# A hybrid attention and recurrence block on one core: the three parked operands of a recurrence head are fetched together instead of one after the other

## The chip, the cores and the metric

The kernel runs on one core of a Trainium2 chip. Its time is the device time of one execution in microseconds (us); lower is better. Besides the time there is one profiled execution, whose trace gives for every instruction its engine, start and duration, and for a waiting engine what it waited for. The engines are PE (matrix multiplication; PEld is its weight load), DVE (vector), ACT (scalar), POOL and SP. A DMA is issued by an engine's instruction queue (SPq, ACTq, POOLq): the issuing instruction stands in the engine's program order with everything else that the engine does.

## The reference

One layer over 512 tokens and 16 meta tokens, model width 2048:

```python
h = rms_norm(x, norm_g)
proj = h @ w_in                       # 2048 -> 12368 columns
(q_a, k_a, v_a, z_a, q_i, k_i, w_i, q_b, f_b, i_b, z_b, gates) = split(proj)
...
o_a = dsa_attention(q, k, v, qi, ki, wi, chunk_ids, topk)     # branch A, 8 heads
y_a = o_a * silu(z_a)
qb = silu(q_b); f = lb + (1 - lb) * sigmoid(f_b); vb = i_b    # branch B, 8 heads of 128
o_b = rms_norm(hgrn2_chunkwise(qb, 1 - f, vb, log(f)), hgrn_out_norm_g)
y_b = o_b * silu(z_b)
merged = sum over the branches of sigmoid(gates) * (y @ w_branch)
return x + merged @ w_out
```

Branch B is a gated linear recurrence: S_t = diag(f_t) S_{t-1} + k_t v_t^T, o_t = S_t^T q_t. For each head it needs the three projections f, q and v, and, after the recurrence, z.

## The kernel before, in words

**Matrix products.** Weights stream from HBM in blocks of 128x1024 elements (tiles `raw`, 512 KB each, a ring of six, DMAs on SP's queue, L381). Each block is split into a high part (`wh`, on ACT, L106) and a low part (`wl`, on DVE, L112), which PE multiplies with the equally split activations. Most blocks belong to pairs: two column groups of 128 are computed with seven block products instead of eight (`run_pair`, L1267). The products carry the names of their PSUM banks: px, py, pv, pz, pw. Sums of weight blocks are made on DVE or by an accumulating DMA on POOL's queue (`raw<-raw`, L121). A product is 24 matmuls of some 256 columns.

**Tasks between the products.** The work that is not a weight product (index scores, top-k, the recurrence, the attention) is written as Python generators, `Task` (L205). A planner (`pump`, L229) is called after every third matmul of a product. It keeps a planned clock for each engine, and lets a task take its next step when the time that the task last yielded, plus a margin of 300 ns, has passed on PE's planned clock. So a yield does not wait on the chip: it decides at build time behind which matmuls the task's next instructions are written. On the chip each engine runs its instructions in that order and waits for semaphores.

**The pairs' order.** First 16 pairs for the recurrence (two for each head: f and q, then v and z), two for the attention's z, eight for the attention's q, k and v, and 16 for the gates; then the products with `w_branch` and `w_out`.

**Parked operands.** SBUF holds 71 tiles of 128x528 (`Slots`). When an operand of a later task is ready and fewer than eight tiles are free, `hold` (L809) writes it to DRAM (tile `held`, on SP's queue, L800) and frees its tile; otherwise it stays. `held` (L817) brings it back: it waits until the store has been written into the program, until a tile is free, then issues the load on ACT's queue (`fetch`, L803, whose DMA line in the profile is L805), and yields the time at which the planner takes it as landed, 4.0 us after the issue on PE's planned clock.

**The recurrence's task.** `hgrn_task` (L981) of head h starts when that of head h-1 is done. It gets f, q and v with three calls of `held`, one behind the other (L984 to L986). Then it transposes v on PE (rows `phl<-ident` and `phv<-ident`; the operand is printed as v, or as r where it was not parked), makes k = 1 - f on ACT (`hk<-f`) and q*f on DVE (`QA<-q,f`), multiplies k and q on PE (`phd`), and goes through seven levels on PE and DVE (`phl<-QA,hk`), a state update (`phs`) and the output (`pho`). The gate of a finished head (`gate_task`, L1105) fetches that head's z in the same way. The attention's tasks `ka_task` and `va_task` fetch xk and xv; they begin when the recurrence's last head is done, the softmax part `pv_task` (`pov`) comes behind them. When the eighth `pv_task` is done, `y_task` loads the branch outputs back (`yr`, on ACT's queue).

Of the kernel before, what the change touches and what calls it, by code (L numbers as in the profile page):

```python
# [30 lines left out]
WAIT = object()  # L31
# [157 lines left out]
def hybrid_kernel(ctx, tc, x, meta, vecs, w_in, rows, w_branch, w_out,  # L189
                  ident_d, tab_q, tab_a, tab_i, masks_d, out):  # L190
    nc = tc.nc
# [5 lines left out]
    E = Core(nc)  # L197
# [70 lines left out]
    def room(n, first=False):  # L268
        while len(S.free) < n + (0 if first else keep[0]):
            yield WAIT  # L270
# [6 lines left out]
    def slot(name, dt=F32):  # L277
        return S.get(name, dt)
# [23 lines left out]
    for c in range(2):  # L302
        s = wp.tile([128, 1024], F32, name=f"xm{c}", tag=f"wh{c}")
# [499 lines left out]
    def fetch(name, of, q, n=512):  # L803
        s = slot(name)
        q.dma_start(s[:, :n], of[:, :n])  # L805
        E.wr[s.tensor.name] = (E.clk["pe"] + 4000.0, "dma")
        return s
# [9 lines left out]
    def held(name, x):  # L817
        s, d, t, n = x
        if s is None:
            while not t.done:  # L820
                yield WAIT
            yield from room(1)
            s = fetch(name, d, nc.scalar, n)
            yield E.wr[s.tensor.name][0]
        return s

    small = [cp.tile([128, 16], F32, name=f"small{i}") for i in range(2)]
    SC = 128.0 ** -0.5

# [137 lines left out]
    hg = {}  # L967
# [13 lines left out]
    def hgrn_task(h, prev):  # L981
        while not LB or not mask_t[0].done or (prev and not prev.done):
            yield WAIT
        f = yield from held("f", hg[h]["f"])  # L984
        q = yield from held("q", hg[h]["q"])
        vx = yield from held("v", hg[h]["v"])  # L986
        yield from room(3)
        at = AT[0]
        k, vt = slots("hk", 2)
# [4 lines left out]
        for c in range(4):  # L994
            e = E.tr(pb[:, 128 * c:128 * c + 128], vx[:, 16 + 128 * c:144 + 128 * c], ident)
# [8 lines left out]
        for c in range(4):  # L1004
            e = E.mm(pb[:, 128 * c:128 * c + 128], k[:, 16 + 128 * c:144 + 128 * c], q[:, 128 * c:128 * c + 128],
                     True, True)
# [7 lines left out]
        for li, m in enumerate(LEVELS):  # L1014
# [5 lines left out]
            for c in range(4):  # L1020
                for j in range(128 // w):
                    e = E.mm(pb[w * j:w * j + ns, 64 * c + w // 2 * j:64 * c + w // 2 * (j + 1)],
                             k[:, 16 + 128 * c + w * j:16 + 128 * c + w * j + ns],
                             qv[:, (128 * c + w * j) // (2 * m):(128 * c + w * j) // (2 * m) + nr, 1, :], True, True)
# [8 lines left out]
            if m < 16:  # L1033
                kv = k[:, :528]
                n = 528 // m
                roff = 16 // m
            else:
                kv = k[:, 16:528]
                n = 512 // m
# [7 lines left out]
            e = E.tt(qv[:, :, 1, :], qv[:, :, 1, :], tr_[:, :, 0:1].to_broadcast([128, 256 // m, m]), OP.mult)  # L1047
            e = E.tt(tt_[:, nxt:nxt + n // 2], tv[:, :, 0], tv[:, :, 1], OP.mult)
# [6 lines left out]
        for c in range(3):  # L1055
            e = E.tr(pb[:, 128 * c:128 * c + 128], k[:, 16 + 128 * c:144 + 128 * c], ident)
# [4 lines left out]
        e = E.act(kd[:, :384], pb[:, :384], AF.Copy)  # L1061
# [4 lines left out]
        for c in range(3):  # L1066
            e = E.mm(pb[:, 128 * c + 128:128 * c + 256], kd[:, 128 * c:128 * c + 128],
                     vt[:, 128 * c:128 * c + 128], True, True)
# [4 lines left out]
        for c in range(3):  # L1073
            e = E.stt(ss[:, 128 * c + 128:128 * c + 256], ss[:, 128 * c:128 * c + 128],
                      tt_[:, toff + c:toff + c + 1], pb[:, 128 * c + 128:128 * c + 256], OP.mult, OP.add)
# [4 lines left out]
        for c in range(4):  # L1080
            cs = slice(128 * c, 128 * c + 128)
            E.mm(po[:, cs], at[:, cs], vt[:, cs], True, False)
            e = E.mm(po[:, cs], qa[:, cs], ss[:, cs], False, True)
# [5 lines left out]
        r = sq[:, 512:528]  # L1089
# [3 lines left out]
        e = E.ptt(r[:, 8:12], r[:, 4:8], mhalf[:, 0:4], OP.pow)  # L1093
        yield e
        e = E.tt(on[:, :512].rearrange("p (b d) -> p b d", b=4), pv, r[:, 8:12, None].to_broadcast([128, 4, 128]),
                 OP.mult)
# [77 lines left out]
    def r_ib(h):  # L1174
        def f(s):
            hg[h]["v"] = hold(s)
            hg_tasks.append(spawn(hgrn_task(h, hg_tasks[-1] if hg_tasks else None), 1))
        return f
# [599 lines left out]
    for u, un in enumerate(units):  # L1778
        d = int(un[1])
# [64 lines left out]
    for half in range(2):  # L1844
        n = (272, 256)[half]
# [154 lines left out]
```

## Time and profile before

| | us |
|---|---|
| median of three runs | 1530.59 |
| lowest and highest of them | 1528.60 and 1531.83 |
| the profiled execution's own time | 1529.07 |
| its span from the first to the last instruction | 1527.3 |
| PE busy in that span | 1500.9 |
| DVE, ACT, POOL busy | 1201.0, 712.5, 165.9 |

The span and the busy times are read from the head of the page; a busy time sums the instructions of one engine, so the difference to the span is the time in which that engine did nothing. For PE that is 26.4 us. The granted clock of PE was 0.999 of full speed over the whole span.

### The profile page before, as it was taken

What the parts mean: (1) busy time and instruction counts of PE and PEld (TensorE: products, weight loads), DVE (VectorE), ACT (ScalarE), POOL (GpSimd) and SP (SyncE); (2) the same over time, 40 slices, a digit from 0 to 9 for tenths busy, and PEclk for the clock granted to TensorE, in tenths of its full rate; (3) what the DMA queues carried; (4) which work ended last, traced back from release to release, by engine and by line L of the source; (5) the groups of instructions that cost most, each with busy time, mean ns of one, the idle gap of its engine ahead of it and who ended that gap; (6) DMA issues with size and microseconds to landing.
All of it is one profiled execution on the core that took longest, in us unless ns stands there. A gap on an engine that the chain in (4) does not pass through costs nothing.

```text
span 1527.3 us, 31296 instructions
## 1 busy us (share of the span) xinstructions
PE 1500.9 (98%) x12756; PEld 1435.2 (94%) x12756; DVE 1201.0 (79%) x2013; ACT 712.5 (47%) x1079; POOL 165.9 (11%) x180
## 2 busy tenths in 40 slices
PE   7999999999999999999999999999999999999998
PEld 6888889999999999999999999999999799989998
DVE  6699899999977787787768768768756768898765
ACT  5565444444434444434554554554454544444342
POOL 2100010010001001011101101101010000002221
PEclk9999999999999999999999999999999999999999
DMA  9323448766666585758677677676678767748883
GB/s 266 83 70 83 110 103 196 187 168 166 162 172 164 148 190 137 185 131 198 142 192 181 156 192 180 161 191 166 164 203 195 228 188 188 212 123 217 214 214 90
DMA packets 300288, 256.50 MB, mean 168 GB/s; under 512 B 11828, under 2 KB 262208, under 8 KB 300144
## 3 DMA queue, kind: packets, MB, share of 16 engines
q1 hardware_dynamic: 271392, 177.44, 40.0%
q0 software_dynamic: 15616, 56.71, 21.3%
q10 hardware_dynamic: 13136, 20.35, 4.2%
q8 instruction: 100, 1.64, 0.5%
q14 instruction: 44, 0.36, 0.1%
HBM read 169.11 MB, written 28.73 MB: 130 GB/s over the span
## 4 chain that ended last, share of the span: by engine, by line
PE 86%; DVE 8%; DMA 2%; issue 2%; ACT 2%; ACTq 0%; SPq 0%; POOL 0%; DVEq 0%
PE pz L96 16%; PE px L96 16%; PE pg L98 12%; PE po L96 10%; PE pv L96 8%; PE pw L96 8%; PE py L96 8%; DVE wl L112 2%; PE phl L98 1%; PE pov L96 1%; PE psc L98 1%; PE plg L98 1%; PE pho L98 1%; ACT wh L106 1%; DVE tk L697 1%
## 5 line engine op out<-in xcount | busy, mean ns | idle before, releaser
L106 ACT ACTIVATE wh<-raw 128x1024 fp32r<-128x1024 f32 x416 | 440.1, 1059 | 557.7 <-PE pz L96 148.9
L112 DVE TENSOR_TENSOR wl<-raw,wh 128x1024 fp32r<-128x1024 f32 x414 | 508.3, 1228 | 148.1 <-ACT wh L106 144.7
L121 POOL DMA_DIRECT2D raw<-raw x108 | 95.0, 993 | 969.0 <-DVE raw L112 678.3
L96 PE MATMUL px<-hH,wh 128*128 128x272 f32 (+1 forms) x672 | 194.6, 290 | 1.3 <-ACT p L106 1.3
L96 PE MATMUL px<-hL,wh 128*128 128x272 f32 (+1 forms) x672 | 192.1, 286 | 0.0
L96 PE MATMUL px<-hH,wl 128*128 128x272 f32 (+1 forms) x672 | 192.1, 286 | 0.0
L96 PE MATMUL po<-wh,mh 128*128 128x256 f32 x896 | 158.5, 281 | 0.5 <-DVE xq L112 0.5
L96 PEld LDWEIGHTS po<-wh,mh 128*128 128x128 f32 x896 | 137.3, 189 | 0.8 <-DVE xq L112 0.7
L112 DVE TENSOR_TENSOR raw<-raw,raw 128x1024 f32<-128x1024 f32 x108 | 132.0, 1222 | 1.8
L96 PEld LDWEIGHTS px<-hH,wh 128*128 128x128 f32 x672 | 126.9, 189 | 2.1 <-ACT p L106 1.6
L96 PEld LDWEIGHTS px<-hL,wh 128*128 128x128 f32 x672 | 126.9, 189 | 0.0
L96 PEld LDWEIGHTS px<-hH,wl 128*128 128x128 f32 x672 | 126.8, 189 | 0.0
L96 PE MATMUL pw<-tT,wh 128*128 128x256 f32 x672 | 126.4, 287 | 0.0
L96 PE MATMUL po<-wl,mh 128*128 128x256 f32 x448 | 125.7, 280 | 0.0
L96 PE MATMUL pv<-tT,wh 128*128 128x256 f32 x672 | 125.1, 285 | 0.0
L96 PE MATMUL pz<-tT,wh 128*128 128x256 f32 x672 | 124.3, 284 | 0.2 <-ACT wh L106 0.2
L96 PEld LDWEIGHTS pz<-tT,wh 128*128 128x128 f32 x672 | 103.2, 189 | 0.9 <-ACT wh L106 0.4
L96 PEld LDWEIGHTS pv<-tT,wh 128*128 128x128 f32 x672 | 103.0, 189 | 0.5
L96 PEld LDWEIGHTS pw<-tT,wh 128*128 128x128 f32 x672 | 103.1, 189 | 0.2
L96 PE MATMUL pz<-hH,wh 128*128 128x256 f32 x336 | 97.3, 289 | 2.9 <-DVE r L112 2.9
L96 PE MATMUL py<-hH,wl 128*128 128x256 f32 x336 | 94.8, 282 | 1.9 <-DVE wl L112 1.9
L96 PE MATMUL py<-hH,wh 128*128 128x256 f32 x336 | 95.9, 286 | 0.0
(349 smaller groups left out, 3582.9 us busy)
## 6 DMA issues: line engine op xcount, KB each, us to landing
raw<-in_w_in_dram SPq DMA_DIRECT2D x192, 512.0 KB, 6.1
raw<-raw POOLq DMA_DIRECT2D x108, 512.0 KB, 6.0
raw<-in_w_branch_dram SPq DMA_DIRECT2D x32, 512.0 KB, 6.3
raw<-in_w_out_dram SPq DMA_DIRECT2D x32, 512.0 KB, 6.5
gd<-r SPq DMA_DIRECT2D x32, 256.0 KB, 2.0
gate<-gd SPq DMA_DIRECT2D x32, 256.0 KB, 6.2
held<-r SPq DMA_DIRECT2D x19, 264.0 KB, 4.0
held<-r SPq DMA_DIRECT2D x18, 256.0 KB, 2.0
```

The lines of the kernel that those rows point to most:

```text
L96: self.nc.tensor.matmul(out, lhsT, rhs, start=start, stop=stop, skip_group_check=True)
L98: self.nc.tensor.matmul(out, lhsT, rhs, start=start, stop=stop)
L106: self.nc.scalar.activation(out, in_, f, **kw)
L112: self.nc.vector.tensor_tensor(out, a, b, op=op)
L121: self.nc.gpsimd.dma_start(out, a, accum_op=OP.add)
L697: e = E.dve([w], [src, m8], kq, lambda v: v.match_replace(w, m8, src, NEG))
```

## The change

A new helper gets any number of parked operands at once. It waits until the stores of all of them stand in the program and until as many tiles are free as operands are parked, issues all loads on ACT's queue one directly behind the other, and yields once, with the latest of their planned landing times.

```diff
+    def held_all(*xs):
+        for _, (s, d, t, n) in xs:
+            while s is None and not t.done:
+                yield WAIT
+        yield from room(sum(x[0] is None for _, x in xs))
+        r, e = [], 0.0
+        for name, (s, d, t, n) in xs:
+            if s is None:
+                s = fetch(name, d, nc.scalar, n)
+                e = max(e, E.wr[s.tensor.name][0])
+            r.append(s)
+        yield e
+        return r
...
     def hgrn_task(h, prev):
         while not LB or not mask_t[0].done or (prev and not prev.done):
             yield WAIT
-        f = yield from held("f", hg[h]["f"])
-        q = yield from held("q", hg[h]["q"])
-        vx = yield from held("v", hg[h]["v"])
+        f, q, vx = yield from held_all(("f", hg[h]["f"]), ("q", hg[h]["q"]), ("v", hg[h]["v"]))
         yield from room(3)
```

ACT's queue at the start of the recurrence's head 1, before: L805 are the loads of parked operands (f, q and v of this head, z of head 0), `wh` the high parts of weight blocks, `r` and `p` evictions of pair products.

```order
L805 DMA f_3684<-held_3012 128x528
L805 DMA z_3686<-held_2689 128x512
L106 ACTIVATE wh_3691<-raw_3385 128x1024
L106 ACTIVATE r_278_3694<-px_3578 128x272
L106 ACTIVATE wh_3727<-raw_3387 128x1024
L805 DMA q_3753<-held_2971 128x512
L106 ACTIVATE wh_3770<-raw_3421 128x1024
L106 ACTIVATE wh_3804<-raw_3464 128x1024
L805 DMA v_3810<-held_3330 128x528
```

The same place on ACT in the changed kernel:

```order
L805 DMA f_3679<-held_3029 128x528
L805 DMA q_3681<-held_2991 128x512
L805 DMA v_3683<-held_3342 128x528
L805 DMA z_3685<-held_2689 128x512
L106 ACTIVATE wh_3693<-raw_3389 128x1024
L106 ACTIVATE r_280_3696<-px_3585 128x272
L106 ACTIVATE wh_3731<-raw_3391 128x1024
L106 ACTIVATE hk_3755<-f_3679 128x528
```

q now stands directly behind f instead of four instructions after it, and v two behind f instead of eight. The first use of f (`hk`) is three instructions behind the last load, with two weight blocks in between; before, it came only in row 291 of ACT, 13 behind f, with six weight blocks in between. The line of the load is L805 in both, since the new helper stands behind it.

PE's queue where that head's v is transposed, before (`phl` and `phv` are the transposes, `py` a pair's product):

```order
L96 MATMUL py_3881<-hH_265,wl_3805 128x256
L102 MATMUL phl_2452<-ident,v_3810 16x128
L102 MATMUL phv_3889<-ident,v_3810 128x128 x4
L96 MATMUL py_3881<-hH_289,wh_3804 128x256
L96 MATMUL py_3881<-hL_290,wh_3804 128x256
```

And in the changed kernel, where the same transposes stand in an earlier product, `pz` of the weight block `wh_3652`:

```order
L96 MATMUL pz_3734<-tT_1778,wl_3653 128x256
L102 MATMUL phl_2452<-ident,v_3683 16x128
L102 MATMUL phv_3758<-ident,v_3683 128x128 x4
L102 MATMUL pht_3766<-ident,on_3550 128x128 x4
L96 MATMUL pz_3734<-tT_1949,wh_3652 128x256
```

The transposes have moved from PE's row 1980 to its row 1903, and the transpose of head 0's output (`pht`) has come to stand beside them. All of the recurrence moves so, by more with every head: v of head 7 is transposed in row 4133 before and in row 3810 now, and the attention's last `pov` moves from row 7725 to 7583. From row 7738 on PE's rows are the same in both. PE has 10587 rows in both programs, DVE 1895 and POOL 185; ACT has 1103 instead of 1104 and SP 424 instead of 425, because one operand less is parked over the whole kernel (36 instead of 37). Of the recurrence's 24 operands 18 are fetched in either program: eight f, six q and four v before, five f, six q and seven v now. Before, ten loads waited for another load of the same head; now none does.

## The prediction, made before the changed kernel ran

> **What bounds the kernel now.** I read the head of the page first, then the chain of work that ended last:
>
> ```profile
> span 1527.3 us, 31296 instructions
> PE 1500.9 (98%) x12756; PEld 1435.2 (94%) x12756; DVE 1201.0 (79%) x2013; ACT 712.5 (47%) x1079; POOL 165.9 (11%) x180
> ...
> PE 86%; DVE 8%; DMA 2%; issue 2%; ACT 2%; ACTq 0%; SPq 0%; POOL 0%; DVEq 0%
> ```
>
> PE is the bound: it does nothing for only 1527.3 - 1500.9 = 26.4 us. The change leaves PE's instructions as they are and only writes them in another order (the same 10587 rows). So it can gain no more than the idle time of PE in the stretch whose order changes. That stretch begins with the first load of a parked operand, at 243.54 us (its row is below), and ends with the attention's last `pov`; from PE's row 7738 on the orders agree. The view of stretches gives busy time by engine (PE, PEld, DVE, ACT, POOL) for both:
>
> ```profile
> 229.00:1132.00 903.00, 897.32 (x8625) 878.08 (x8625) 711.21 (x1260) 417.97 (x631) 93.58 (x110) 1.00 0.70 171
> 1132.00:1527.00 395.00, 385.95 (x2873) 366.81 (x2872) 292.67 (x359) 174.42 (x216) 50.91 (x45) 1.00 0.71 190
> ```
>
> In the stretch PE is idle for 903.00 - 897.32 = 5.68 us at a granted clock of 1.00. The waits of PE in it name the reasons:
>
> ```profile
> PE pz L96 <- DVE r L112: 1.4, 1, 1.4
> PE px L96 <- ACT p L106: 1.3, 1, 1.3
> PE pov L96 <- ACT pT L106: 0.9, 3, 0.5
> PE pka L102 <- DMA xk<-held: 0.6, 1, 0.6
> PE phd L98 <- ACT hk L106: 0.6, 2, 0.3
> PE pva L102 <- DMA xv<-held: 0.3, 1, 0.3
> ```
>
> Only the fifth row, 0.6 us in two heads, belongs to the recurrence. The loads that the change puts together never made PE wait: no row names f, q or v.
>
> **What it removes.** Ten loads no longer wait for another load of their head. For head 1 the time line shows what that chain took:
>
> ```profile
> 315.38 0.33 ACTq L805 DMA_DIRECT2D f<-held  x1
> 315.74 1.79 ACTq L805 DMA_DIRECT2D z<-held  x1
> 321.20 0.33 ACTq L805 DMA_DIRECT2D q<-held  x1
> 327.41 0.33 ACTq L805 DMA_DIRECT2D v<-held  x1
> 333.47 0.27 PE L102 MATMUL phl<-ident,v 128*16 128x128 f32 x1
> ```
>
> q is issued 5.82 us behind f, v 6.21 us behind q, and PE transposes v 6.06 us after that. Ten such steps of about 6 us (an estimate from these two) are some 60 us by which the recurrence can end earlier (the order's rows of head 7 move the same way). But in those 60 us PE worked: it ran the pairs' products, which lay in the queue anyway. The serial loads were hidden behind them, so their end gains nothing directly: **0 us**. What is late next is what was late before, PE's own work. At the other end, an earlier attention would matter only if something waited for it; PE's order there is unchanged, and its row of waits in the tail (shown below) names a weight block, not the attention.
>
> **What it adds on ACT.** Each load holds ACT for 0.33 us (rows above), as before; their number is 18 again. New is that v of head 0 now stands directly behind f, and must wait for its own store:
>
> ```profile
> 241.39 0.82 SPq L800 DMA_DIRECT2D held<-r  x2
> 243.52 1.06 ACT L106 ACTIVATE wh<-raw 128x1024 fp32r<-128x1024 f32 x1 [0.21 <-DVE raw L112]
> 243.54 0.36 ACTq L805 DMA_DIRECT2D f<-held  x1
> 245.69 1.06 ACT L106 ACTIVATE wh<-raw 128x1024 fp32r<-128x1024 f32 x1 [1.11 <-PE py L96]
> 251.55 2.85 PE pz L96 x24
> ...
> 286.07 1.17 SPq L800 DMA_DIRECT2D held<-r  x2
> ...
> L112 DVE TENSOR_TENSOR wl<-raw,wh 128x1024 fp32r<-128x1024 f32 x414 | 508.3, 1228 | 148.1 <-ACT wh L106 144.7
> ...
> held<-r SPq DMA_DIRECT2D x19, 264.0 KB, 4.0
> ```
>
> The second store is out by 242.2 us and lands, at the page's median of 4.0, near 246.2. ACT then starts the block of 245.69 about 0.9 us late (246.2 + 0.33 against 245.69). Queued behind it are that `wh`, its `wl` on DVE, and PE's pz that uses both at 251.55. With 1.06 for the `wh` and 1.23 for the `wl` the block is ready before 249.5. That leaves 2 us, so PE does not see it: **0 us**. For head 1 the last stores go out at 286.07, 29 us ahead of f at 315.38; the heads after it start as late behind their stores.
>
> **What it adds on the DMA engines.** Here is the one unknown. f, q and v now start within 0.7 us, while the planner still counts 4.0 us for all of them. So PE reaches the transpose of v about 6.06 us after the loads were issued, as measured from the last load of head 1. The trace shows no three loads together; it shows pairs, f with z (the first three rows head 1, the next two head 3, then all eight f):
>
> ```profile
> f<-held ACTq DMA_DIRECT2D x1, 264.0 KB, 4.9
> v<-held ACTq DMA_DIRECT2D x1, 264.0 KB, 5.6
> z<-held ACTq DMA_DIRECT2D x1, 256.0 KB, 8.3
> ...
> f<-held ACTq DMA_DIRECT2D x1, 264.0 KB, 2.6
> z<-held ACTq DMA_DIRECT2D x1, 256.0 KB, 3.0
> ...
> DMA to landing us min/median/max: 2.6/2.7/4.9
> ```
>
> From below: in a quiet moment a second load lands 0.4 us later than the first (3.0 against 2.6); a third, by the same step, needs 0.66 + 3.4 = 4.1 us from f's issue, and PE waits for nothing. From above: beside weight loads z needed 8.3; v in its place, issued 0.66 after f, lands after 9.0 us, 2.9 behind PE. Six heads have v behind another load (0, 1, 2, 3, 4 and 6): 0 to 17 us. The nearest row is the attention's, where two parked operands are fetched together already:
>
> ```profile
> 1019.83 0.33 ACTq L805 DMA_DIRECT2D xk<-held  x1
> 1020.20 1.05 ACTq L805 DMA_DIRECT2D xv<-held  x1
> 1025.73 0.63 PE L102 MATMUL pka<-ident,xk 128*128 128x128 f32 x4 [0.64 <-DMA xk<-held]
> 1026.61 0.66 PE L102 MATMUL pva<-ident,xv 128*128 128x128 f32 x4 [0.26 <-DMA xv<-held]
> ```
>
> PE waits 0.64 + 0.26 = 0.90 us in this one of three such places (the waits above have no other). But f started in a quiet moment in seven heads of eight (median 2.7, one 4.9), so I take one wait in eight: 6 x 0.90 / 8 = **0.7 us**. The Trainium skill, in "DMA: Bandwidth & Descriptors", section "Issuing engines are not separate DMA queues", speaks against the change: DMAs of all issuing engines run on the same 16 DMA engines and interleave. By that page's fit for one DMA, 2.0 us and the bytes at 436 GB/s, three loads of 784 KB would take 3.8 us when alone, an estimate that lies beside my 4.1; the 8.3 us of z is what interleaving costs in this trace.
>
> **What it moves.** The tasks meet other products, so the remaining waits fall elsewhere. Nothing in the trace makes them rarer or more frequent; I keep the 5.68 us.
>
> **Sum.** Span 1527.3 + 0 + 0 + 0.7 = 1528.0. The profiled execution took 1529.07, 1.5 below the median of the three runs (1530.59); on the median's scale the forecast is 1530.59 + 0.7 = **1531.3 us**. A run can tell about 0.2%, 3.1 us, from no change.
>
> **The rivals.**
> *Late v (slower).* The three loads meet the weight loads and v lands behind PE's transpose, in all six heads with the 0.90 us measured for xk and xv: 5.4 us, **1536.0**. It decides once v needs more than 6.06 us. For it: v alone needed 5.6 in head 1, only half a microsecond less. Against it: the quiet start of f. A long wait costs more than itself, as the one in the tail shows:
>
> ```profile
> PE pg L98 <- DVE wl L112: 2.2, 1, 2.2
> ...
> 1207.00:1210.00 3.00, 0.78 (x4) 0.32 (x3) 3.00 (x6) 3.00 (x6) 0.00 (x0) 1.00 0.03 10
> 1210.00:1213.00 3.00, 3.00 (x8) 2.34 (x9) 3.00 (x6) 3.00 (x7) 0.00 (x0) 0.50 0.66 217
> 1213.00:1216.00 3.00, 3.00 (x14) 2.41 (x13) 3.00 (x6) 3.00 (x7) 0.85 (x1) 0.93 0.41 144
> ```
>
> After 2.2 us of idle the granted clock is 0.50 for 3 us and 0.93 for three more: 1.5 + 0.2 us lost, 3.9 in all. The waits of 1.3 and 1.4 us left it at 1.00. The Trainium skill, "TensorE: Matmul & The Clock Gate", section "HAM oscillation — how this bites in real kernels", wants gaps of more than about 3.4 us for that; here 2.2 us was enough, so the measured gap decides.
> *One new long wait (slower).* A task in its new place holds up one weight block as in the tail: 3.9 us, **1535.2** with the 0.7.
> *Better luck (faster).* The long wait in the tail goes with the shift of the loads before it (3.9) and a fifth of the 5.68: 5.0 us, **1525.6**. Against it: the orders there agree.
> *It changes nothing.* Where operands are not parked the helper does nothing; if that held mostly, the time would be **1530.6**. Eighteen loads speak against it.
>
> **How the numbers follow.** Forecast 0.55; late v 0.18; one new long wait 0.08; better luck 0.15; nothing 0.04. Forecast and nothing are within 0.2%, so the same has 0.59, slower 0.26, faster 0.15. The range runs from 1526 (5 us of the 5.68 gone) to 1537 (late v with a microsecond to spare); past it lie half of better luck and the upper bound of 17 us, together under 0.2.
>
> **What would show it.** In the profile after: PE's instructions as before and idle time in the changed stretch of 5 to 8 us; f, q and v issued within 0.7 us and landing within 6; no row of PE's waits for f, q or v above 1 us. A row `phl` or `phv` waiting for `v<-held` in several heads would be late v; a granted clock below 1.00 between 229 and 1132 us would be a long wait; no 2.2 us row for `pg` would be better luck.

## The result and the profile after

| | before | changed |
|---|---|---|
| median of five runs, us | 1530.52 | 1546.78 |
| lowest and highest | 1527.50 and 1531.83 | 1545.61 and 1547.15 |
| ratio, 95% interval | | 1.0110 [1.0095, 1.0125] |

The changed kernel is slower by 1.1%. The forecast was 1531.3 in a range of 1526 to 1537; the time lies outside it, on the side of the rival "late v", but three times as far as that rival's price (16.3 us slower, where it had 5.4). The head of the page of the changed kernel, the changed stretch (busy time of PE, PEld, DVE, ACT, POOL, then the granted clock, the DMA share and GB/s) and PE's waits in it:

```profile
span 1543.8 us, 31290 instructions
PE 1505.4 (98%) x12756; PEld 1439.3 (93%) x12756; DVE 1199.6 (78%) x2013; ACT 713.1 (46%) x1079; POOL 168.5 (11%) x180
```

```profile
229.00:1132.00 903.00, 884.47 (x8463) 863.92 (x8462) 697.77 (x1247) 410.79 (x621) 95.66 (x110) 0.99 0.68 166
```

```profile
PE phl L102 <- DMA v<-held: 6.9, 2, 3.9
PE phl L98 <- DVE QA L112: 2.2, 4, 1.2
PE pka L102 <- DMA xk<-held: 2.1, 1, 2.1
PE pqa L102 <- DMA xq<-held: 1.9, 1, 1.9
...
PE phd L98 <- DMA q<-held: 0.6, 1, 0.6
```

The span grew by 16.5 us. PE's idle time accounts for 12.0 of that (38.4 against 26.4) and its busy time for 4.5, with the same instructions. The idle time arose in the changed stretch, 903.00 - 884.47 = 18.5 us against 5.7 before, and the list of waits opens with names that were not in it: v, the recurrence's QA and q, and the attention's xq; xk's wait grew from 0.6 to 2.1. A row gives the total, the number of waits and the longest: PE stood 3.9 us for one v. The page's chain of waits says the same in one figure: 5% of the span went through DMA, before 2%.

The long wait is in head 1, the head that the prediction worked with. The time line of ACT's queue, the DMA groups of 316 to 328 us (last column: us from issue to landing) and PE's row:

```profile
316.81 0.33 ACTq L805 DMA_DIRECT2D f<-held  x1
317.16 0.79 ACTq L805 DMA_DIRECT2D q<-held  x1
317.99 1.35 ACTq L805 DMA_DIRECT2D v<-held  x1
319.38 1.60 ACTq L805 DMA_DIRECT2D z<-held  x1
```

```profile
raw<-in_w_in_dram SPq DMA_DIRECT2D x4, 512.0 KB, 8.2
raw<-raw POOLq DMA_DIRECT2D x2, 512.0 KB, 7.1
f<-held ACTq DMA_DIRECT2D x1, 264.0 KB, 5.0
v<-held ACTq DMA_DIRECT2D x1, 264.0 KB, 8.4
q<-held ACTq DMA_DIRECT2D x1, 256.0 KB, 8.3
z<-held ACTq DMA_DIRECT2D x1, 256.0 KB, 7.9
```

```profile
326.41 0.38 PE L102 MATMUL phl<-ident,v 128*16 128x128 f32 x1 [3.90 <-DMA v<-held]
```

PE was ready at 326.41 - 3.90 = 322.5, 5.7 us behind f's issue. v was issued 1.18 us behind f (q's issue held ACT for 0.79, not 0.33) and took 8.4, so it landed 9.6 us behind f's issue. PE waited for nothing else between 312 and 345 us. While PE stood, ACT ran nearly dry (0.17 us busy in 324 to 327), and behind the wait PE's clock fell; the windows around this wait and around head 4's (3.0 us, ending at 483.6):

```profile
324.00:327.00 3.00, 0.59 (x3) 0.60 (x4) 2.73 (x5) 0.17 (x1) 0.00 (x0) 0.89 1.00 329
327.00:330.00 3.00, 3.00 (x18) 3.00 (x17) 1.43 (x4) 0.09 (x1) 0.00 (x0) 0.54 1.16 311
...
483.00:486.00 3.00, 2.40 (x12) 2.41 (x13) 0.70 (x2) 0.86 (x2) 0.00 (x0) 0.55 1.14 313
```

The last but one column is the mean busy share of the sixteen DMA engines (it adds up the packets' times, so it can pass 1): while v was outstanding they were full. Behind each wait PE is granted 0.54 or 0.55 of its clock for three microseconds, so its matmuls count as busy for longer.

### The profile page after: what moved, and what is told of

Read it like the earlier page. It is cut to its first block, busy times and chain, and to the rows that moved or that the text cites. A ratio compares the mean times of both kernels' runs of the same rounds, so it can differ in the third digit from the quotient of the medians.

```text
span 1543.8 us, 31290 instructions
## 1 busy us (share of the span) xinstructions
PE 1505.4 (98%) x12756; PEld 1439.3 (93%) x12756; DVE 1199.6 (78%) x2013; ACT 713.1 (46%) x1079; POOL 168.5 (11%) x180
## 4 chain that ended last, share of the span: by engine, by line
PE 83%; DVE 8%; DMA 5%; issue 2%; ACT 2%; ACTq 0%; POOL 0%; SPq 0%; DVEq 0%; POOLq 0%
PE px L96 15%; PE pz L96 15%; PE pg L98 12%; PE po L96 10%; PE pw L96 7%; PE py L96 7%; PE pv L96 7%; DVE wl L112 2%; PE phl L98 1%; DMA z<-held 1%; PE plg L98 1%; PE psc L98 1%; PE pov L96 1%; ACT wh L106 1%; DMA v<-held 1%
```

## The experiments

The kernels were timed in three sessions, on three chips, each beside the kernel before on the same chip; its median there was 1529.11, 1528.55 or 1529.23 us, and kernels of different sessions are compared by their ratio to it. My first theory was the **lead**: the change shortened the time from a load's issue to its use, since 4.0 us are planned for three loads where 4.0 were planned for each, and it is the planned 4.0 that is too short. Rivals were that the concurrent loads themselves cost time, that an operand landed late only because v came last, and that the moved tasks meet other waits whatever the lead.

### The three loads together, 8.0 us planned

```diff
 def held_all(*xs):
-        yield e
+        yield e + 4000.0
```

> The three loads together as in the changed kernel, but the task goes on 8.0 us after them on the planner's clock, not 4.0. Theory late landing: v landed 8.4 and 6.5 us after its issue (9.6 and 8.2 after that of f) where PE came for it after 5 to 6, so 4 us more cover it. The waits of the recurrence on v, q and QA (6.9 + 0.6 + 2.2 us) go, the clock stays at 1.00 there, and the time falls from 1546.8 by 11 to 15 us, to 1532 to 1536; the attention keeps its own waits. Rival misplaced work: the recurrence costs more wherever it is written more densely, not by the landing; then the time stays above 1542. Rival contention: the loads themselves slow the weight blocks; then PE waits for wl or wh appear or stay and the time stays above 1542.

Measured 1531.70 against 1529.11, ratio 1.0021 [1.0012, 1.0030]. The loads still start together and land as late as in the changed kernel (v took 7.4 us in head 1 and 8.0 in head 3), but most of the loss is gone. What is left of PE's waits for v, QA and xk:

```profile
PE phl L98 <- DVE QA L112: 1.8, 4, 0.7
...
PE phl L102 <- DMA v<-held: 0.2, 1, 0.2
...
PE pka L102 <- DMA xk<-held: 0.7, 1, 0.7
```

Loads that start together thus cost little by themselves; the use that comes ahead of their landing does. The waits for xk and xq are gone too, but for 0.7 us, although their own 4.0 us were not touched: the recurrence's last output (`pho`) comes at 682 us, as before (679) and not at 652 as in the changed kernel, and the attention's tasks fall near their old places.

### Only the single loads, 8.0 us planned

```diff
 def held(name, x):
-            yield E.wr[s.tensor.name][0]
+            yield E.wr[s.tensor.name][0] + 4000.0
```

> The changed kernel, with 8.0 us instead of 4.0 for the single loads only (xk, xv, xq of the attention and z of a finished head); f, q and v as changed. Theory late landing: the attention's waits on xk, xq and xv (2.1 + 1.9 + 0.3 us) and the clock lost behind the one for xq (1.5 us) go: 1546.8 falls by 4 to 7 us, to 1540 to 1543; the waits for v stay. Rival: the attention's part of the loss is only other places met by chance; then these waits turn up under other names and the time stays within 2 us of 1546.8.

Measured 1550.75, ratio 1.0142 [1.0127, 1.0157]: not the gain that the theory expected, but a further loss. The waits for xk, xq and xv went and those for v stayed (6.8 us in two), but others came under new names, as the rival had it: 3.1 us in the attention's stretch (a product `pv`, for DVE's `pTM`), and 5.3 us behind it. PE's row and ACT's time line there:

```profile
1166.46 0.55 PE L96 MATMUL pz<-hH,wh 128*128 128x256 f32 x1 [5.30 <-DVE r L112]
```

```profile
1154.33 9.21 ACTq L1488 DMA_DIRECT2D yr<-yd  x6
1163.67 2.95 ACT L106 ACTIVATE wh<-raw 128x1024 fp32r<-128x1024 f32 x3 [9.74 <-DMA yr<-yd]
```

Issuing six of the loads with which `y_task` brings the branch outputs back held ACT's queue for 9.2 us, with weight blocks queued behind them; DVE's next `wl` waited for those, and the `r` that PE needed stood behind that `wl`. The kernel before has such a row too (9.66 us at 1188.01), but there PE's only wait up to 1215 us is one of 2.2. So a task's place decides how far that blockage is felt.

### Both, 8.0 us planned

```diff
-            yield E.wr[s.tensor.name][0]
+            yield E.wr[s.tensor.name][0] + 4000.0
...
-        yield e
+        yield e + 4000.0
```

> 8.0 us for the three loads together and for all single loads. Theory late landing: nothing in the recurrence or the attention waits for a parked operand any more; 1546.8 falls by 16 to 20 us, to 1527 to 1531, at or a little below the kernel before. Rival misplaced work: above 1540. If both parts add, the gain is the sum of those of the two runs with one part each.

Measured 1526.80, ratio 0.9990 [0.9980, 0.9999]; the same kernel run once more gave 1527.01, ratio 0.9988 [0.9978, 0.9997]:

> The run with the loads together and 8.0 us everywhere once more, beside the others of this call, since its lead over the kernel before (0.1%) was at the edge of its interval. Theory late landing: 1525 to 1529, 0 to 0.2% below the kernel before.

This is the only kernel that came out ahead of the one before, by a tenth of a per cent both times. Each interval only just leaves out 1, and a tenth is less than the 0.2% that the prediction took a run to be able to tell; so no loss is shown, and hardly a gain. The two parts do not add: the first alone won 0.9% against the changed kernel, the second alone lost 0.3%, both together win 1.2%. All of PE's waits between 229 and 680 us are these two, neither for a parked operand:

```profile
PE pz L96 <- ACT wh L106: 1.0, 1, 1.0
PE phl L98 <- DVE QA L112: 0.5, 1, 0.5
```

The loads land no sooner than in the changed kernel: f's median from issue to landing is 6.6 us (5.0 there, 2.7 before), q's 8.0 (5.0 and 6.3).

```profile
f<-held ACTq DMA_DIRECT2D x8, 264.0 KB, 6.6
...
q<-held ACTq DMA_DIRECT2D x6, 256.0 KB, 8.0
```

### v first

```diff
-        f, q, vx = yield from held_all(("f", hg[h]["f"]), ("q", hg[h]["q"]), ("v", hg[h]["v"]))
+        vx, f, q = yield from held_all(("v", hg[h]["v"]), ("f", hg[h]["f"]), ("q", hg[h]["q"]))
```

> The changed kernel, with the loads issued in the order v, f, q instead of f, q, v; the 4.0 us as they are. Theory late landing: v then lands as f did (5.0 and 6.6 us in the two heads that waited), so PE's waits for v shrink to under 2 us in all, but f and q land late instead and PE waits for them one step later, at phd or QA: 2 to 6 us gained, 1541 to 1545. Rival, only v matters because it alone is needed by PE itself: the waits go altogether and the time falls below 1537. Rival, the order of issue is nothing: within 2 us of 1546.8.

Measured 1542.31, ratio 1.0091 [1.0076, 1.0106]. PE's wait for v fell from 6.9 to 1.3 us, but others took its place; of PE's waits between 229 and 680 us these are the first three:

```profile
PE phd L98 <- ACT mt L106: 2.6, 1, 2.6
PE phl L98 <- DVE QA L112: 2.2, 4, 1.2
PE phl L102 <- DMA v<-held: 1.3, 1, 1.3
```

The waits of ACT say what lies behind them (in head 1 `hk` stands ahead of `mt` on ACT, and `phd` needs it):

```profile
ACT hk L106 <- DMA f<-held: 8.7, 4, 3.1
ACT hk L106 <- DMA held<-r: 4.7, 1, 4.7
```

`hk` waits for f, which now lands behind v, and in one head for a store: `hk` is written into a tile that a store (`held<-r`) has given free, and the tile is given free when the store is written into the program, not when it has landed. The order of the three loads cures the wait for v, but what is used next is late too. PE's idle time in this stretch is 8.4 us against 10.9 in the changed kernel; the ratio's interval overlaps that kernel's, [1.0095, 1.0125], so a gain in time is not shown.

### The three loads together, 6.0 us planned

```diff
-        yield e
+        yield e + 2000.0
```

> The changed kernel, with 6.0 us between the three loads together and the task's next step (4.0 in the changed kernel, 8.0 in the run before). Theory late landing: PE comes 2 us later, so of the two waits for v of 3.9 and 3.0 us some 2 and 1 are left and the clock keeps up or nearly so; the time lies between the two, at 1534 to 1540. Rival, a matter of the order alone, with no dose: the time agrees with one of the two, 1532 or 1547, within 2 us.

Measured 1543.14, ratio 1.0092 [1.0077, 1.0108]: less was won than expected, and the interval overlaps the changed kernel's. The waits for v are down to 2.5 us, but seven waits for QA add up to 6.9. The longest, again in head 1, on SP's queue, on DVE and on PE:

```profile
321.10 4.14 SPq L800 DMA_DIRECT2D held<-r  x1
```

```profile
330.93 0.69 DVE L112 TENSOR_TENSOR QA<-q,f 128x512 f32<-128x512 f32 x1 [2.96 <-DMA held<-r]
```

```profile
331.77 0.45 PE L98 MATMUL phl<-QA,hk 128*32 128x16 f32 x32 [2.67 <-DVE QA L112]
```

q was in by 324.9 (issued at 316.52, 8.4 to landing). It was the store again: issued at 321.10 into full DMA engines it took 9.7 us, to 330.8, and QA is written into its tile. So a task that comes too early meets the landing of stores as well as of loads, and 2.0 us more moved the waits on rather than ending them: PE's idle time in 229 to 680 is 11.4 us, against 10.9 in the changed kernel. PE's busy time is 1502.9 us against 1505.4: in this stretch the clock did not drop, not even behind the 2.67 us.

### The serial loads, 2.0 us planned (the kernel before)

```diff
 def held(name, x):
-            yield E.wr[s.tensor.name][0]
+            yield E.wr[s.tensor.name][0] - 2000.0
```

> The kernel before, loads one behind the other, with 2.0 us planned for every load instead of 4.0. It has no three loads together, and its recurrence is written nearly as early as in the changed kernel (PE's row 3896 for the last head's v, against 3810 and 4133 before). Theory short lead: single loads landed 2.6 to 7.0 us after their issue where PE now comes after about 4, so waits on v, q or QA, on xk, xv and xq appear without any three loads together, and the time is 1535 to 1545. Rival, only the loads' concurrence makes them late: the time stays at 1528 to 1533.

Measured 1557.03, ratio 1.0186 [1.0169, 1.0203]. No three loads are issued together here, yet the loss of the changed kernel appears, larger, and above the 1535 to 1545 that the theory expected:

```profile
PE phl L102 <- DMA v<-held: 10.0, 6, 3.6
...
PE pka L102 <- DMA xk<-held: 3.9, 1, 3.9
```

This run doesn't take the overlap of loads away altogether: with 2.0 us planned, all three of head 1 overlap in flight, and in heads 3 to 5 two are issued 0.4 us apart. The clear case is head 0, on ACT's queue and on PE:

```profile
245.48 0.35 ACTq L805 DMA_DIRECT2D v<-held  x1
253.61 0.37 PE L102 MATMUL phl<-ident,v 128*16 128x128 f32 x1 [3.08 <-DMA v<-held]
```

v was issued 2.2 us behind f, which landed 0.6 us later; beyond that v shared the DMA engines with no other parked operand, and it still took 8.0 us. PE came after 5.1. So a short lead is enough for the loss, and three loads together are not needed for it; with the 8.0 us run above, that shows the lead, set against a landing beside the weights, as the cause from both sides.

### The serial loads, 8.0 us planned (the kernel before)

```diff
-            yield E.wr[s.tensor.name][0]
+            yield E.wr[s.tensor.name][0] + 4000.0
```

> The kernel before, loads one behind the other, with 8.0 us planned for every load of a parked operand. Theory late landing: its own waits on xk and xv (0.9 us) go and the recurrence is drawn out; 1527 to 1531, no change against before that can be measured. Rival, the longer plan by itself makes the 2 us by which the run with 8.0 us everywhere and the loads together beat the kernel before: then this one too is at 1525 to 1528. Rival, the drawn out recurrence collides with the attention: above 1533.

Measured 1563.28, ratio 1.0227 [1.0212, 1.0242], far outside what the lead alone would give; the rival named there held. There is not one wait for a parked operand in the recurrence, and none of over 1 us for anything. But its last head ends at 768 us (the last `pho`; 679 before), the attention starts that much later, and the last `pov` comes at 1213.9 instead of 1126.5, when the pairs' products that cover it are used up:

```profile
1150.00:1570.00 420.00, 384.06 (x2731) 359.36 (x2729) 292.40 (x392) 179.49 (x242) 50.57 (x45) 0.95 0.62 170
```

```profile
PE ppt L102 <- ACT lg L106: 7.6, 3, 3.9
PE pg L98 <- ACT yH L106: 4.6, 1, 4.6
PE pqa L102 <- DMA xq<-held: 4.4, 1, 4.4
```

So the serial form cannot be given 8.0 us everywhere, and the concurrent form can: the change buys room that it did not use. Whether the serial form could bear some lead between 4.0 and 8.0 us was not tried.

### z later

The group of head 1 has four loads. In this kernel the gate of a finished head asks for its z 12 us later.

```diff
 def gate_task(h, on):
+        yield E.clk["pe"] + 12000.0
         z = yield from held("z", hg[h]["z"])
```

> The changed kernel, but the gate of a finished head asks for its z 12 us later by the planner's clock, so that z is no longer issued right behind the three operands of the next head. If the fourth load delays v (the DMA engines were busy to nine tenths while f, q, v and z of head 1 landed after 5.0, 8.3, 8.4 and 7.9 us): v of heads 1 and 4 lands some 2 us sooner, PE's two waits for it (3.9 and 3.0 us) fall below 2 us each and no granted clock of about 0.55 follows them, 1537 to 1542. If the three loads with the weight blocks and sums that land beside them are enough: PE waits for v as before, 1544 to 1549.

Measured 1545.10, ratio 1.0102 [1.0085, 1.0118]. z is now issued at 333.71, when v is long in, and lands in 2.7 us instead of 7.9. PE's waits hardly notice:

```profile
325.87 0.38 PE L102 MATMUL phl<-ident,v 128*16 128x128 f32 x1 [3.81 <-DMA v<-held]
...
483.61 0.38 PE L102 MATMUL phl<-ident,v 128*16 128x128 f32 x1 [3.09 <-DMA v<-held]
```

```profile
v<-held ACTq DMA_DIRECT2D x1, 264.0 KB, 7.4
```

v took a microsecond less in head 1 but was issued 2.06 us behind f instead of 1.18; in head 4 it took 6.6 us, 6.5 in the changed kernel. The fourth load isn't the cause: three loads beside weight blocks, two weight sums and a store are enough, and in head 0 of the run with 2.0 us one load was. How much of the 8 us belongs to the weight blocks and how much to POOL's sums was not tried.

### Both, 10.0 us planned

```diff
-            yield E.wr[s.tensor.name][0]
+            yield E.wr[s.tensor.name][0] + 6000.0
...
-        yield e
+        yield e + 6000.0
```

> The changed kernel with 10.0 us planned from the issue of any parked operand's load to its use, for the three together and for single ones. If 8.0 us covered the landing already and only the lead counts: no wait for a parked operand, 1525 to 1529, as with 8.0. If a longer lead draws the recurrence out so that it takes cover from the attention, as it did with serial loads and 8.0 us each: waits of the attention's softmax behind 1150 us and a granted clock below 0.95 there, above 1531.

Measured 1541.29, ratio 1.0077 [1.0062, 1.0092]. PE waits for no parked operand, and the recurrence ends at 687 us. But the last `pov` comes at 1187.7, where with 8.0 it came at 1161.6. Then `yr` goes out too late for the products with `w_branch`; ACT's queue and PE's row:

```profile
1190.14 10.34 ACTq L1488 DMA_DIRECT2D yr<-yd  x8
```

```profile
1201.50 0.80 PE L98 MATMUL pg<-yH,wh 128*128 128x512 f32 x1 [11.29 <-ACT yH L106]
```

One wait of 11.3 us is most of the difference to the run with 8.0 (1539.9 - 1525.1 = 14.8 us of span); behind it the granted clock is 0.80 over 1190 to 1215. Of the three leads tried for all loads with f, q and v together, only 8.0 us is free of both losses: the landing's below, the attention's end above.

## Why the prediction was wrong

**The removed waits: 0 us, right.** The kernel before had no wait for f, q or v in PE's list; taking their chain away gave PE nothing. What it gave to the planner, a recurrence that ends at 652 instead of 679 us (27 us, where the working had some 60), was of no use there.

**v of head 0 behind its own store: 0 us, right.** v of head 0 went out at 243.70, 0.69 us behind f, without the delay to about 246.2 that the working allowed for, and PE's list has no wait in that head.

**The one unknown, v beside f and q: this term failed.** It was sized at one wait of 0.90 us in eight, 0.7 us for the six heads. Two heads of the six waited, for 3.9 and 3.0 us, which is 1.15 us per head in the mean and not 0.12; q and QA add up to 2.8 us more.

The reason given for the one in eight, that "f started in a quiet moment", says little of v. In heads 0, 1 and 3 f landed as before (2.7, 5.0 and 2.7 us; 2.6, 4.9 and 2.6 before), and v behind it took 5.4, 8.4 and 4.3. In head 4, which asked for its loads 9.5 us earlier than before, f too took 6.6 instead of 2.7. Loads together were not late everywhere: v's median is 4.9 us over seven loads, 5.4 over four before. What had gone is the time to spare. Before, PE came 6.06 us behind v's own issue in head 1; now it was ready 4.5 us behind it (5.7 behind f's), and in head 4 3.6 (5.3 behind f's). In head 1 the lead is 1.6 us shorter and the landing 2.8 later (8.4 for 5.6), and 0.5 had been to spare: 1.6 + 2.8 - 0.5 = 3.9 us, the wait.

The bound from above, 9.0 us from f's issue to v's landing, was no extreme: v needed 9.6 in head 1 and 8.2 in head 4. It was exceeded because q's issue took 0.79 us instead of 0.33 (0.5 us more), and the wait grew by PE coming 0.4 us earlier than after a single load. The estimate of 3.8 us, from the fit that the Trainium skill gives in "DMA: Bandwidth & Descriptors", section "Anatomy of one DMA — SWDGE (gpsimd) path", was passed in both heads; the page gives that fit for DMAs issued by POOL, and these loads go by ACT's queue. The other statement of the Trainium skill's page, that DMAs of all issuing engines run on the same 16 engines and interleave, agrees with a DMA share of 1.0 and more in the windows, and it was the one to weigh.

**A long wait costs its clock too: known, but left out of the sum.** The prediction read the drop to 0.50 behind 2.2 us of idle and put it into a rival with a chance of 0.08, as if one such wait were the exception. Three stretches of the changed kernel have it, behind the waits for v in heads 1 and 4 and for xq; each is 38 or 39 us long with a clock of 0.96, so some 1.5 us lost in each, 4.6 together, as much as PE's busy time grew (4.5):

```profile
309.00:347.00 38.00, 34.10 (x381) 33.22 (x380) 32.78 (x62) 14.87 (x20) 4.47 (x5) 0.96 0.62 156
463.00:502.00 39.00, 35.88 (x395) 34.70 (x394) 27.34 (x43) 15.98 (x24) 4.46 (x5) 0.96 0.53 137
1042.00:1081.00 39.00, 36.35 (x283) 35.09 (x282) 24.57 (x44) 18.88 (x32) 3.33 (x4) 0.96 0.66 165
```

**"I keep the 5.68 us": failed by the attention's part.** Its tasks moved with the recurrence, and their own loads of xk and xq landed late in two new places, 2.1 and 1.9 us, where 0.6 stood before. That they moved is what did it: with the recurrence's 8.0 us alone these waits went, at the same 4.0 us for the attention's own loads. The recurrence's rows (6.9 + 2.2 + 0.6) and these (1.5 + 1.9 more than before) make 13.1 us, near the 12.9 by which the stretch's idle time grew; some small waits of before are gone.

**The signs to look for** were the right ones: the forecast's own test, f, q and v in within 6 us, was missed, and rows for v with a clock below 1.00 were both named in advance.

## What to carry to other kernels

When loads are taken out of a chain, the lead of each use shrinks even though nothing is removed: count the time from issue to use that the chain gave for free, and plan the landing time under load, not that of a load alone. Measure it from the slow rows, in which other transfers already fly (here 8.3 us for z, not the 2.7 for f): two of v's seven loads, at 6.5 and 8.4 us, made the waits, and the other five none. And vary the lead in both directions before you judge such a change: 4, 8 and 10 us for all loads gave 1546.8, 1526.8 and 1541.3 here, the first late at the landing, the last late at what follows.

## What the runs showed of the hardware

No sharp limit in idle time shows for the drop of the clock. In the changed kernel it followed a wait of 1.92 us for xq:

```profile
1045.29 0.66 PE L102 MATMUL pqa<-ident,xq 128*128 128x128 f32 x4 [1.92 <-DMA xq<-held]
1042.00:1050.00 8.00, 6.08 (x39) 5.88 (x38) 3.02 (x5) 1.54 (x2) 1.03 (x1) 0.79 0.90 242
```

But the tail's wait of the same kernel, 2.16 us for `wl`, left it at 1.00 in the windows behind, where the same wait of 2.2 us had been followed by 0.50 before:

```profile
1225.00:1228.00 3.00, 0.84 (x5) 0.37 (x3) 3.00 (x6) 3.00 (x6) 0.00 (x0) 1.00 0.03 10
1228.00:1231.00 3.00, 3.00 (x13) 2.48 (x14) 3.00 (x6) 3.00 (x7) 0.00 (x0) 1.00 0.65 208
```

In the traces of all these kernels (the 7 to 8 us ahead of PE's first work left out) the 17 waits of 2.86 us and more were all followed by a granted clock of 0.50 to 0.64 over the next 3 us. Of 30 waits from 1.8 to 2.81 us, 13 were followed by a drop and 17 were not, even at the same place: in the changed kernel xq's wait was (1.92 us) and xk's was not (2.15), with 6.0 us planned xk's was (2.14) and xq's was not (1.86). So below 2.86 us length alone doesn't decide it; what does, these runs leave open. The Trainium skill, in "TensorE: Matmul & The Clock Gate", section "HAM oscillation — how this bites in real kernels", names gaps of more than about 3.4 us. Shorter ones were enough here: 2.2 us in the kernel before, 1.92 and 2.99 in the changed one.

Issuing a DMA can take far longer than the 0.33 us of a quiet one: 0.79, 1.35 and 1.60 us within the four loads of head 1, and 9.2 to 10.3 us for groups of five to eight `yr` loads. What ACT had been given ahead of the loads went on meanwhile (a `wh` ran at 317.46 beside the issue of q and v), but what stood behind them waited: the next `wh` began at 321.03, when z's issue had ended at 320.98.
